# Loads of the gate rows' weights placed behind the weight loads of queries and keys, and forward transforms of a convolution as three rounded products

## The chip, the cores and the metric

The kernel runs on one core of a Trainium2 chip. Its time is the device time of one execution in microseconds; the time before is the median of three. The core has a matrix engine (TensorE, PE in the profile, with its weight loads as PEld), a vector engine (VectorE, DVE), an activation engine (ScalarE, ACT), a general one (GpSimd, POOL), and a sequencer that mostly issues transfers (SyncE, SP). Each engine runs its own instructions in the order in which the program lists them, and semaphores connect them.

## The reference

Two layers work on 256 latent tokens and 256 context tokens of 1024 channels. In both, a token mixer is followed by a squared-ReLU MLP, and each sub-layer is gated and modulated by columns that an adaLN map computes from a conditioning vector:

```python
def adaln(cvec, w, b):
    return jnp.split(jax.nn.silu(cvec) @ w + b, 6, axis=-1)   # shift, scale, gate, twice

def sq_relu_mlp(u, w1, w2):
    return jnp.square(jax.nn.relu(u @ w1)) @ w2
...
x <- LN(ALPHA*x + gate * F(x*(1+scale)+shift))
```

Layer 0's mixer is a conformer convolution: a product to 2048 channels (pw1), a sigmoid gate, a depthwise convolution over 31 taps, layer norm, silu, and a second product (pw2). Context tokens are convolved as one sequence, latent tokens in rows of 64. Layer 1's mixer is a bidirectional chunkwise mLSTM: it makes up-projections (x and z), a short convolution `xc`, values from the former (wv), queries and keys from `xc` (wq, wk), then scores and outputs. All is in 32-bit floats.

## The kernel before

Channels lie on partitions and tokens on the free axis. The order of the work on PE is: pw1, the depthwise convolution, pw2, the four chunks of layer 0's MLP, the up-projections, values, queries and keys (in two pairs of heads, `pair`), attention, and layer 1's MLP.

**Rounded products.** Most matrix products are done as three products of rounded 32-bit operands: each operand is split into a high part, made by a cast on ACT, and a low part, made by a subtraction on DVE (`split`, lines 155 and 156); then come high by high, high by low and low by high (`mm3`, lines 186 to 190). A weight comes in by a 1 MB load on SP's queue into one of three `raw` tiles (`raw_load`, L149); its split gives two `wh` and two `wl` tiles of 128 by 1024, each of which has four buffers.

**The convolution.** The depthwise convolution is done by a transform along the tokens. `turn` (transposes on PE, line 909, and a copy on ACT, line 910) and `vturn3` (a transpose on DVE, a store to memory and a load back, line 904) put the gated tensor with tokens on partitions into `A`. `fwd` (line 926) multiplies `A` by tables of sines and cosines; for the two context tiles (`tt < 2`) it takes windows of the tokens, for which the table `F0` is masked by rows (`ge32`, `lt32`, `ge96`). These are products of plain 32-bit operands, six per half of the channels. `products` multiplies the spectrum by that of the taps, `back` transforms back. The two halves of the channels follow each other, the first at about 69 us, the second at about 135 us.

**The adaLN columns of layer 1.** The class `AdaV` (`step` and `load`, line 420 on) works them out on DVE: each step takes a block `ar` of 256 KB of the transposed map, loaded on SP's queue (L446) into one of two buffers, multiplies it by the row of conditioning values and sums (L439: one custom instruction and one that reads the accumulator). `ada_n1` has units 0 to 3 (32 blocks), `ada_n2` the units 6 to 9, then 4, 5, 10, 11 (64 blocks). The last four are the gates, which two ACT transfers then put into memory as rows (`gate_rows`, L1257). The program calls the steps of `ada_n2` within the loops of values, queries and keys.

**What sets the order.** A scheduler arranges the instructions of each engine; a block in `tc.issue_after(instruction)` is kept behind the instruction named. As nothing holds the `ar` loads, all 96 were moved ahead, into layer 0's MLP, where four or five stand on SP's queue between one weight load and the next.

In that MLP (`mlp`, line 1184 on), PE does for each chunk first the product with w1, whose result passes ACT (relu, L1207), DVE (square, L1208) and a `split` into `hid` (L155, L156), then that with w2. The last chunk's w2 goes through `gemm2` with some of its weights kept in tiles named `u`.

## Time and profile before

| | |
|---|---|
| time, median of 3 runs | 1650.22 us (1646.95 to 1651.23) |
| profiled execution | 1650.45 us |
| its span, first to last instruction | 1648.7 us |
| PE busy | 1623.7 us (98%) |
| DVE busy | 1077.0 us (65%) |
| ACT busy | 728.1 us (44%) |
| mean granted TensorE clock | 0.992 |
| loads `ar`, issued from and to | 164.8 to 509.9 us, 96 of them |

Times are counted from the span's start. A row of the timeline gives start, duration, engine, line and operation, then in brackets how long the engine had been idle and what released it. A row of the windows gives for a stretch the busy time of each engine and the number of instructions, then the granted clock of TensorE (1 is full speed), the share of the DMA engines that was busy, and the GB/s. A row of the waits gives who waited for whom, the total in us, how often, and the longest.

### The profile page before, as it was taken

How to read it: one execution, taken by the hardware profiler on the slowest of the kernel's cores; microseconds unless marked ns; L12 is line 12 of the kernel's file. 1: busy time of each engine (PE TensorE's matmuls, PEld its weight loads, DVE VectorE, ACT ScalarE, POOL GpSimd, SP SyncE). 2: the span in 40 equal slices, each digit the busy share in tenths (PEclk: the TensorE clock that was granted, in tenths of full speed). 3: DMA queues.
4: the chain of work that ended last, by engine and by line, in shares of the span. 5: the costliest groups of instructions: out<-in, count | busy, mean ns of one | idle time of the engine just before them, and what ended most of it. 6: DMA issues, size and time to landing. Idle time of an engine off the chain costs nothing.

```text
span 1648.7 us, 22836 instructions
## 1 busy us (share of the span) xinstructions
PE 1623.7 (98%) x8754; PEld 1356.6 (82%) x8754; DVE 1077.0 (65%) x2052; ACT 728.1 (44%) x1173; POOL 15.2 (1%) x67
## 2 busy tenths in 40 slices
PE   9999999999996999999999999999999999999998
PEld 6675998888885998887777899898888888888887
DVE  7697886986756676763233643453389876787777
ACT  4214763322314376652222532442378654555453
POOL 0000000000000000000000000000000000000001
PEclk9999999999998999999999999999999999999999
DMA  9766233555655157578654632343375566745552
GB/s 361 250 220 239 103 115 128 197 190 193 201 176 153 52 164 226 188 242 281 220 188 149 238 128 103 107 175 131 136 258 187 209 230 203 255 182 190 191 192 90
DMA packets 91069, 306.88 MB, mean 186 GB/s; under 512 B 15020, under 2 KB 33360, under 8 KB 63312
## 3 DMA queue, kind: packets, MB, share of 16 engines
q1 hardware_dynamic: 66416, 289.12, 50.2%
q10 hardware_dynamic: 24544, 16.30, 3.2%
q8 instruction: 69, 1.13, 0.3%
q14 instruction: 40, 0.33, 0.1%
HBM read 287.52 MB, written 17.87 MB: 185 GB/s over the span
## 4 chain that ended last, share of the span: by engine, by line
PE 90%; DMA 6%; DVE 3%; issue 1%; ACT 0%; DVEq 0%; SPq 0%; ACTq 0%
PE mm L186 15%; PE mm L189 15%; PE mm L190 15%; PE mm L202 10%; DMA ar<-adaT_w 4%; PE mm L228 4%; PE mm L230 3%; PE mm L229 3%; PE cv L230 2%; PE cv L228 2%; PE cv L229 2%; PE fl L360 1%; DMA raw<-w 1%; DVE ar L439 1%; PE ln L228 1%; PE ln L229 1%
## 5 line engine op out<-in xcount | busy, mean ns | idle before, releaser
L156 DVE TENSOR_TENSOR wl<-raw,wh 128x1024 fp32r<-128x1024 f32 (+1 forms) x344 | 416.5, 1215 | 255.4 <-ACT wh L155 250.5
L155 ACT CAST wh<-raw 128x1024 fp32r<-128x1024 f32 (+1 forms) x344 | 357.0, 1045 | 458.8 <-PE mm L189 269.0
L189 PE MATMUL mm<-u,wh 128*128 128x512 f32 (+1 forms) x802 | 288.7, 361 | 0.0
L186 PE MATMUL mm<-u,wh 128*128 128x512 f32 (+1 forms) x674 | 239.3, 356 | 0.0
L190 PE MATMUL mm<-u,wl 128*128 128x512 f32 (+1 forms) x674 | 238.1, 355 | 0.0
L189 PEld LDWEIGHTS mm<-u,wh 128*128 128x128 f32 x802 | 151.2, 189 | 23.0 <-issue 0.8
L186 PEld LDWEIGHTS mm<-u,wh 128*128 128x128 f32 x674 | 127.2, 189 | 20.5 <-issue 2.4
L190 PEld LDWEIGHTS mm<-u,wl 128*128 128x128 f32 x674 | 127.1, 189 | 18.5 <-issue 0.8
L186 PE MATMUL mm<-hid,wh 128*128 128x512 f32 (+1 forms) x256 | 95.1, 372 | 13.4 <-ACT hid L155 13.3
L186 PE MATMUL mm<-xm,wh 128*128 128x512 f32 x256 | 100.2, 391 | 0.0
L190 PE MATMUL mm<-xm,wl 128*128 128x512 f32 x256 | 99.6, 389 | 0.0
L189 PE MATMUL mm<-hid,wh 128*128 128x512 f32 (+1 forms) x256 | 94.8, 370 | 0.7 <-DVE hid L156 0.7
L190 PE MATMUL mm<-hid,wl 128*128 128x512 f32 (+1 forms) x256 | 94.5, 369 | 0.0
L228 PE MATMUL mm<-wh,xl 128*128 128x512 f32 x208 | 81.5, 392 | 1.0 <-ACT xl L155 1.0
L229 PE MATMUL mm<-wh,xl 128*128 128x512 f32 x208 | 81.2, 390 | 0.0
L230 PE MATMUL mm<-wl,xl 128*128 128x512 f32 x208 | 80.4, 391 | 0.0
L189 PE MATMUL mm<-qq,wh 128*128 128x272 f32 x256 | 73.9, 289 | 0.0
L186 PE MATMUL mm<-qq,wh 128*128 128x272 f32 x256 | 73.5, 288 | 0.0
L190 PE MATMUL mm<-qq,wl 128*128 128x272 f32 x256 | 73.5, 288 | 0.0
L186 PEld LDWEIGHTS mm<-hid,wh 128*128 128x128 f32 x256 | 50.1, 196 | 21.6 <-ACT hid L155 14.1
L1373 DVE SCALAR_TENSOR_TENSOR E<-pad,vecs,E 128x512 f32<-128x512 f32 x64 | 48.0, 750 | 27.3 <-ACT E L1371 26.0
L155 ACT CAST hid<-E 128x256 fp32r<-128x256 f32 (+1 forms) x70 | 33.9, 485 | 67.9 <-DVE E L1208 64.4
(595 smaller groups left out, 3245.9 us busy)
## 6 DMA issues: line engine op xcount, KB each, us to landing
raw<-w SPq DMA_DIRECT2D x64, 1024.0 KB, 4.9
raw<-wo SPq DMA_DIRECT2D x32, 1024.0 KB, 4.9
ar<-adaT_w SPq DMA_DIRECT2D x96, 256.0 KB, 3.0
raw<-ada_w SPq DMA_DIRECT2D x20, 1024.0 KB, 7.4
raw<-wv SPq DMA_DIRECT2D x16, 1024.0 KB, 6.3
raw<-wq SPq DMA_DIRECT2D x16, 1024.0 KB, 4.8
raw<-wk SPq DMA_DIRECT2D x16, 1024.0 KB, 4.8
u<-wqT SPq DMA_DIRECT2D x56, 256.0 KB, 5.7
```

Of the source, the lines that this page charges most:

```text
L155: c = nc.scalar.copy(hi, src)
L156: lastsub[0] = nc.vector.tensor_tensor(lo, src, hi.bitcast(F32), op=ALU.subtract).ins
L186: a = nc.tensor.matmul(ps, wh, xh, start=start, stop=False)
L189: nc.tensor.matmul(ps, wh, xl, start=False, stop=False)
L190: lastmm[0] = nc.tensor.matmul(ps, wl, xh, start=False, stop=stop).ins
L202: nc.tensor.matmul(o_, w_, x_, start=start and i == 0, stop=stop and i == 15)
L228: nc.tensor.matmul(ps, xh, wh, start=start, stop=False)
L229: nc.tensor.matmul(ps, xl, wh, start=False, stop=False)
L230: return nc.tensor.matmul(ps, xh, wl, start=False, stop=stop).ins
L360: a = mark_unit[0] = nc.tensor.matmul(ps[32 * j:32 * j + 32], cs[:, kt, 14 - 2 * v:46 - 2 * v], blocks[kt], start=first and kt < 4, stop=l ...
L439: nc.vector.tensor_tensor_reduce(tmp("S") if s == 0 else w, w, crow[s][half], 1.0, o if half else V(f"ada_b{self.l}", col), op0=ALU.mult, ...
L1373: nc.vector.scalar_tensor_tensor(s2_(acc), pad[:, :, k:k + C], V("w_conv", m * QTAP + k), s2_(acc), op0=ALU.mult, op1=ALU.add)
```

## The change

It has two parts and some smaller moves.

First, the loads of `AdaV` whose unit stands behind the first four in its list, that is the 32 blocks for the gates, are kept behind the last weight load that the program has issued at that point. Their place is thereby in the stage of queries and keys, and their two instructions each on DVE, and the two transfers `g_dr` on ACT, follow them there.

Second, the context's forward transforms become three rounded products. The tables are split into `FH` and `FL`, masked on DVE instead of POOL; `A`'s two context tiles are split into high and low parts (`a_parts`, held in `U` tiles), from the transposes' result in `turn` and from `A` in `a_split`. `fwd` then issues 18 rounded matmuls per half where it issued six plain ones, in a fixed order.

Beside these, the first half of the block `second` is loaded into `F` tiles, since the `U` tiles are taken, two groups of loads are kept behind it, and two orders near the transposes of silu are fixed.

```diff
--- before.py
+++ after.py
@@ -381,7 +381,7 @@
             else:
                 for i in range(4):
                     t = make()
-                    nc.sync.dma_start(t, ada_w[l, u, half, :, i * 512:(i + 1) * 512])
+                    mark["load"] = nc.sync.dma_start(t, ada_w[l, u, half, :, i * 512:(i + 1) * 512]).ins
                     ts.append(t)
         return ts
 
@@ -443,7 +443,8 @@
         def load(self):
             n, kt = divmod(self.i, DT)
             w = adp.tile([P, 512], F32, tag="ar", name=nm("ar"), bufs=2)
-            nc.sync.dma_start(w, adaT_w[self.units[n], kt // 2, kt % 2])
+            with tc.issue_after(loaded[0]) if n > 3 else nullcontext():
+                nc.sync.dma_start(w, adaT_w[self.units[n], kt // 2, kt % 2])
             self.i += 1
             return w
 
@@ -796,18 +797,22 @@
     (nc.vector.tensor_scalar(cf, cf, -1.0 / L, 2.0 / L, op0=ALU.mult, op1=ALU.add))
     nc.vector.tensor_scalar(tab[:, L:3 * L], tab[:, L:3 * L], cf, None, op0=ALU.mult)
 
-    def masked(name, zero):
-        t = padp.tile([P, L], F32, name=name)
-        nc.gpsimd.tensor_copy(t, F0)
-        for a_, b_ in zero:
-            nc.gpsimd.memset(t[a_:b_, :], 0.0)
-        return t
-
-    ge32 = masked("ge32", [(0, 32)])
-    lt32 = masked("lt32", [(32, 64), (64, 128)])
-    ge96 = masked("ge96", [(0, 64), (64, 96)])
-
-    WIN = [[(F0[0:96, :], 0)], [(ge32, 0), (lt32, 1)], [(ge96, 0), (F0[0:96, :], 1)], [(ge32, 1)]]
+    FH, FL = [padp.tile([P, L], F32R, name=n_) for n_ in ("FH", "FL")]
+    split(FH, FL, F0)
+    mc = padp.tile([P, 3], F32, name="mc")
+    for i_, c_ in enumerate((31.5, 95.5)):
+        nc.vector.tensor_scalar(mc[:, i_:i_ + 1], p_, c_, None, op0=ALU.is_gt)
+    nc.vector.tensor_scalar(mc[:, 2:3], mc[:, 0:1], -1.0, 1.0, op0=ALU.mult, op1=ALU.add)
+
+    def masked(name, i_):
+        ts = [padp.tile([P, L], F32R, name=name + n_) for n_ in "hl"]
+        for t, f_ in zip(ts, (FH, FL)):
+            nc.vector.tensor_scalar(t, f_.bitcast(F32), mc[:, i_:i_ + 1], None, op0=ALU.mult)
+        return ts
+
+    ge32, ge96, lt32 = [masked(n_, i_) for i_, n_ in enumerate(("ge32", "ge96", "lt32"))]
+    F96 = [FH[0:96, :], FL[0:96, :]]
+    WIN = [[(F96, 0)], [(ge32, 0), (lt32, 1)], [(ge96, 0), (F96, 1)], [(ge32, 1)]]
     with tc.issue_after(lastload[0]):
         nc.sync.dma_start(bdw, bdw_d.broadcast_to([P, D]))
     behind.__exit__(None, None, None)
@@ -887,7 +892,16 @@
         else:
             vturn3(f, a)
 
-    turns, three = [], []
+    turns, three, aparts = [], [], {}
+
+    def a_parts(h):
+        if h not in aparts:
+            aparts[h] = [[U(F32R) for _ in range(2)] for _ in range(2)]
+        return aparts[h]
+
+    def a_split(h):
+        for t in range(2):
+            split(*[a_[t][:, 0:2 * P] for a_ in a_parts(h)], A[:, t, h * 512:h * 512 + 2 * P])
 
     def vturn3(f, a):
         h, m = divmod(f, 4)
@@ -902,12 +916,16 @@
             if h == 0:
                 with tc.issue_after(loaded[0]):
                     nc.sync.dma_start(A[:, :, 0:2 * P], a_dr[0])
+                a_split(0)
 
     def turn(f, a):
         tr = psum("ln")
         for b in range(4):
             mark["tr"] = nc.tensor.transpose(tr[:, b * P:(b + 1) * P], a[:, b * P:(b + 1) * P], ident).ins
-        nc.scalar.copy(A[:, :, f * P:(f + 1) * P], tr.rearrange("p (b c) -> p b c", b=4))
+        sl = slice(f % 4 * P, f % 4 * P + P)
+        for t in range(2):
+            split(*[a_[t][:, sl] for a_ in a_parts(f // 4)], tr[:, t * P:(t + 1) * P])
+        nc.scalar.copy(A[:, 2:4, f * P:(f + 1) * P], tr[:, 2 * P:4 * P].rearrange("p (b c) -> p b c", b=2))
         if f == 3:
             with tc.issue_after(mark["tr"]):
                 ada_g1.mm(first, range(4, 8))
@@ -926,18 +944,20 @@
     def fwd(h, tt, xfs):
         sl = slice(h * 512, (h + 1) * 512)
         ps_[tt] = [], list(xfs[::-1])
-        for b in (1, 0) if tt < 2 else (0, 1):
+        a = None
+        for b in (0, 1) if tt > 1 and h == 0 else (1, 0):
             if tt < 2:
-                w_ = WIN[2 * tt + b]
+                w_ = [(fm[k], a_parts(h)[q][t]) for k, q in ((0, 0), (1, 0), (0, 1)) for fm, t in WIN[2 * tt + b]]
                 for i, (fm, t) in enumerate(w_):
-                    a = nc.tensor.matmul(xfs[b], fm, A[0:fm.shape[0], t, sl], start=i == 0, stop=i == len(w_) - 1)
+                    with tc.issue_after(a.ins) if a else nullcontext():
+                        a = nc.tensor.matmul(xfs[b], fm, t[0:fm.shape[0], :], start=i == 0, stop=i == len(w_) - 1)
             else:
 
                 def half_():
                     r = slice(64 * b, 64 * b + 64)
                     return nc.tensor.matmul(xfs[b], F0[r, :], A[r, tt, sl], start=True, stop=True,
                                             tile_position=(64 * b, 0))
-                if b == 0:
+                if b == h:
                     a = lead = half_()
                 else:
                     with tc.issue_after(lead.ins):
@@ -1036,6 +1056,7 @@
         if m == 8:
             with tc.issue_after(mark["gate"]):
                 nc.scalar.dma_start(A[:, :, 512:512 + 2 * P], a_dr[1])
+            a_split(1)
         if m == 4:
             blocks = ada_load(0, 5)
             with tc.issue_after(lastmm[0]):
@@ -1079,8 +1100,9 @@
     gemm(pw1, range(6), u, T, pw1_next, pre=pre1, ahead=True)
     for g in range(2):
         pre_pw2(g)
-    last = ada_load(0, 8)
-    second = ada_load(0, 7, U)
+    second = ada_load(0, 7, F, (0,)) + ada_load(0, 7, U, (1,))
+    with tc.issue_after(mark["load"]):
+        last = ada_load(0, 8)
     with tc.issue_after(mark["tr"]):
         ada_mm(ada_s2.ps, second, 1, False, False, range(4))
     for tt in range(2):
@@ -1102,14 +1124,17 @@
     late4 = []
     for i, tag in enumerate("SLSL"):
         late4.append(tmp(tag))
-        nc.sync.dma_start(late4[i], ada_w[0, 9, 1, :, i * 512:(i + 1) * 512])
+        with tc.issue_after(mark["load"]):
+            nc.sync.dma_start(late4[i], ada_w[0, 9, 1, :, i * 512:(i + 1) * 512])
     more += late4
     with tc.issue_after(mark["fwd", 2]):
         ada_mm(ada_s2.ps, last, 2, False, False)
         ada_mm(ada_s2.ps, more, 3, False, False)
     lead2 = [psum(), psum("cv")]
-    with tc.issue_after(mark_unit[0].ins):
+    filled = {0: mark_unit[0].ins}
+    with tc.issue_after(filled[0]):
         ada_mm(ada_s2.ps, second, 1, False, False, range(4, 8))
+    filled[2] = mark_unit[0].ins
     sact = {0: [], 1: []}
 
     def silu(s):
@@ -1120,9 +1145,10 @@
                 if s == 0 and f == 4:
                     with tc.issue_after(mark["turn", 3]):
                         gate2_sums()
+                    filled[4] = mark_unit[0].ins
                 for i in (1, 3, 0, 2):
                     k = f + i // 2
-                    with tc.issue_after(mark_unit[0].ins) if s == 0 and f == 4 else nullcontext():
+                    with tc.issue_after(filled[f]) if s == 0 and f < 6 else nullcontext():
                         mark["turn", k] = nc.tensor.transpose(tr[:, i * P:(i + 1) * P],
                                                               Y[2 * s + i % 2][k // 4][:, k % 4 * P:k % 4 * P + P], ident).ins
             y = tmp("S")[:, LO]
```

**SP at the end of layer 0's MLP.** `raw` are weight tiles, `w_0` the MLP's weights; the number in a name counts the tiles, which differs by some between the kernels. Before, the last three weight loads and what stands ahead of them:

```order
L446 DMA ar_9807<-adaT_w 128x512
L446 DMA ar_9868<-adaT_w 128x512
L149 DMA raw_4663<-w_0 128x2048
L446 DMA ar_9953<-adaT_w 128x512
L446 DMA ar_10060<-adaT_w 128x512
L446 DMA ar_10169<-adaT_w 128x512
L446 DMA ar_10276<-adaT_w 128x512
L446 DMA ar_10385<-adaT_w 128x512
L149 DMA raw_4727<-w_0 128x2048
L446 DMA ar_10492<-adaT_w 128x512
L446 DMA ar_10601<-adaT_w 128x512
L149 DMA raw_4823<-w_0 128x2048
```

Now, the weight loads of the same place:

```order
L149 DMA raw_4294<-w_0 128x2048
L447 DMA ar_8105<-adaT_w 128x512
L149 DMA raw_4358<-w_0 128x2048
L149 DMA raw_4437<-w_0 128x2048
L149 DMA raw_4513<-w_0 128x2048
L149 DMA raw_4589<-w_0 128x2048
L149 DMA raw_4663<-w_0 128x2048
L149 DMA raw_4728<-w_0 128x2048
L149 DMA raw_4792<-w_0 128x2048
L149 DMA raw_4888<-w_0 128x2048
```

The blocks `ar` between the weight loads are gone from there, but for one.

**SP and DVE at the start of the queries.** `xc_8128` before is `xc_8193` now: the eight subtractions into `xc` make the low parts of the last quarter of the input of the queries and keys; `rk` are rows of gate weights, `res` is the transposed values' tile. DVE before:

```order
L156 TENSOR_TENSOR wl_8233<-raw_8202,wh_8232 128x1024
L1414 STREAM_TRANSPOSE res_8037<-vt_8071 128x16x32
L156 TENSOR_TENSOR xc_8128<-raw_8126,xc_8128 128x256
L156 TENSOR_TENSOR xc_8129<-raw_8126,xc_8129 128x256
L156 TENSOR_TENSOR xc_8134<-raw_8126,xc_8134 128x256
L156 TENSOR_TENSOR xc_8135<-raw_8126,xc_8135 128x256
L156 TENSOR_TENSOR xc_8140<-raw_8126,xc_8140 128x256
L156 TENSOR_TENSOR xc_8141<-raw_8126,xc_8141 128x256
```

DVE now:

```order
L156 TENSOR_TENSOR wl_8298<-raw_8267,wh_8297 128x1024
L1440 STREAM_TRANSPOSE res_8102<-vt_8136 128x16x32
L439 ISA ar_8372,ada_94<-ar_8372,L_2806,ada_94 128x512
L439 ISA ada_94 128x1
L439 ISA ar_8433,ada_94<-ar_8433,L_2805,vecs 128x512
L439 ISA ada_94 128x1
L156 TENSOR_TENSOR xc_8193<-raw_8191,xc_8193 128x256
L156 TENSOR_TENSOR xc_8194<-raw_8191,xc_8194 128x256
L156 TENSOR_TENSOR xc_8199<-raw_8191,xc_8199 128x256
L156 TENSOR_TENSOR xc_8200<-raw_8191,xc_8200 128x256
L156 TENSOR_TENSOR xc_8205<-raw_8191,xc_8205 128x256
L156 TENSOR_TENSOR xc_8206<-raw_8191,xc_8206 128x256
```

SP now, at that place:

```order
L149 DMA raw_8267<-wq 128x2048
L447 DMA ar_8325<-adaT_w 128x512
L149 DMA raw_8330<-wq 128x2048
L1488 DMA rk<-wg_d 128x256
L447 DMA ar_8372<-adaT_w 128x512
L149 DMA raw_8375<-wq 128x2048
L447 DMA ar_8433<-adaT_w 128x512
L149 DMA raw_8438<-wq 128x2048
```

Two blocks now stand on DVE ahead of the first `xc` subtraction; the second of them, `ar_8433`, stands on SP behind two weight loads and `ar_8372`.

## The prediction

> **What bounds the kernel now.** I read the page's first and fourth parts, then PE's waits, then the stretches around the one large wait, then what released it.
>
> ```profile
> PE 1623.7 (98%) x8754; PEld 1356.6 (82%) x8754; DVE 1077.0 (65%) x2052; ACT 728.1 (44%) x1173; POOL 15.2 (1%) x67
> ...
> PE 90%; DMA 6%; DVE 3%; issue 1%; ACT 0%; DVEq 0%; SPq 0%; ACTq 0%
> ```
>
> PE is busy for 98% of the span. So an edit can pay in two ways: by removing PE's own work, or by filling the few places where it stands still. The waits (engine, line waited for, us in total, times, longest) say where these are:
>
> ```profile
> PE mm L186 <- ACT hid L155: 13.3, 2, 12.1
> PE cv L180 <- DVE ones L139: 1.1, 1, 1.1
> ```
>
> One wait of 12.1 us stands out, and the next is 1.1. Its place is the end of layer 0's MLP. In windows (PE's busy us and instructions first, then the other engines; behind them the granted clock, the DMA share and GB/s):
>
> ```profile
> 510.00:520.00 10.00, 9.90 (x51) 8.27 (x49) 8.14 (x14) 5.09 (x9) 0.00 (x0) 1.00 0.37 125
> 520.00:530.00 10.00, 0.60 (x3) 0.30 (x2) 2.22 (x3) 1.10 (x2) 0.00 (x0) 0.67 0.66 89
> 530.00:535.00 5.00, 1.64 (x6) 1.35 (x7) 3.02 (x5) 3.67 (x7) 0.00 (x0) 0.50 0.58 243
> 535.00:540.00 5.00, 3.77 (x18) 3.47 (x18) 2.88 (x7) 1.09 (x2) 0.00 (x0) 0.50 0.76 257
> 540.00:550.00 10.00, 10.00 (x71) 10.00 (x71) 2.99 (x7) 0.00 (x0) 0.00 (x0) 0.81 0.20 83
> 550.00:560.00 10.00, 10.00 (x84) 9.95 (x83) 7.01 (x18) 3.13 (x8) 0.00 (x0) 1.00 0.00 0
> ```
>
> PE's idle time there is 0.10 + 9.40 + 3.36 + 1.23 = 14.1 us. Moreover the clock fell to half, and the work done at half clock lost as much again as full speed would have taken less: 0.2 + 0.82 + 1.89 us up to 540, and then 13 of 84 matmuls in 10 us (1.5 us) to 0.19 of 10 us (1.9 us). The place costs 14.1 + 4.4 to 4.8, about 18.6 us.
>
> Why does PE stand? Timeline rows of SP, DVE and ACT, and the chain of waits:
>
> ```profile
> 495.35 0.33 SPq L149 DMA_DIRECT2D raw<-w  x1
> 496.63 9.85 SPq L446 DMA_DIRECT2D ar<-adaT_w  x5
> 507.28 0.33 SPq L149 DMA_DIRECT2D raw<-w  x1
> 518.43 0.33 SPq L149 DMA_DIRECT2D raw<-w  x1
> ...
> 505.36 0.75 DVE L439 CUSTOM_DVE_ANT_0 ar<-ar,L,ada 128x512 f32<-128x512 f32 x1 [1.57 <-DMA ar<-adaT_w]
> 506.03 1.22 DVE L156 TENSOR_TENSOR wl<-raw,wh 128x1024 fp32r<-128x1024 f32 x1
> ...
> 520.52 0.59 ACT L1207 ACTIVATE E<-mm 128x512 f32<-128x512 f32 x1
> 531.34 1.14 ACT L155 CAST u<-raw 128x512 fp32r<-128x512 f32 x2 [10.23 <-DMA raw<-w]
> 532.38 0.61 ACT L155 CAST hid<-E 128x512 fp32r<-128x512 f32 x1
> ...
> 507.28 5.47 DMA raw<-w
> 518.43 12.82 DMA raw<-w
> ```
>
> SP needs 9.85 us for five `ar` loads, since each waits for a buffer that DVE frees one step later. DVE in turn stands in front of an `ar` (1.57 us idle) while `wl` waits behind it. So the last weight load went out at 518.43 and needed 12.82 us. The cast of `hid`, on which PE waits, stands on ACT behind the casts `u` of that weight, and so it started at 532.38, although the activation ahead of it was over at 521.1.
>
> **The change part by part: the end of the MLP.** Nearly all `ar` loads leave this place. The last weight load then waits only for its `raw` buffer, and that is freed by the subtraction `wl` of the load three places ahead, which needs a `wl` buffer that PE frees. PE takes 24 matmuls for one `wh`, 24 x 0.227 = 5.4 us by the product's pitch (quoted below as 0.23), so a load is needed every 10.9 us. From the order I place the buffer four `wh` ahead at about 509, cast and subtraction behind it (1.05 and 1.22) and the load at about 511.8. With 5.47 us it lands at 517.3, ahead of the activation at 520.52. The `u` casts are then done before `hid` comes up. The chain that is left is the last activation to the last `hid` subtraction. Its steps are activation 0.59, square 0.7, cast 0.62, subtraction 0.69, with some waiting between them: from 520.52 to about 523.5 or 524. PE's last w1 matmul ends at 519.9, and it has about 2 us of matmuls on the other `hid` tiles, as it did in the 3.77 us of the window 535 to 540. I take 2 us left of the hole, with no drop of the clock. **Gain 18.6 − 2 = about 16.5 us**; bounds 12.5 (the hole is left at 6 us, if the load lands like the one that took 12.82) and 18.6 (nothing left).
>
> The 32 × 0.83 us of DVE work moves too, and is free at its old place as PE bounds the stage.
>
> **The context's transforms.** Chain rows (start, us, what), and DVE's row of the turn before the first half:
>
> ```profile
> 61.82 0.23 PE mm L189
> 66.41 1.00 PE fl L360 x8
> 67.40 0.59 PE ln L909 x4
> 68.99 5.35 PE mm L933 x12
> 135.31 4.92 PE mm L933 x11
> ...
> 66.45 0.75 DVE L882 SCALAR_TENSOR_TENSOR E<-mm,vecs,E 128x512 f32<-128x512 f32 x1 [2.99 <-PE mm L190]
> ```
>
> The six plain matmuls of a half stand as twelve records and take 5.35 us, that is 0.89 each; a rounded one takes 0.23 (0.227 as the mean over a longer run of them). Eighteen take 4.1 us, so 1.25 less per half and 2.5 for both. In the new order the third output needs a product bank that `products` frees on DVE; I put 0.3 us per half on this. The new splits on ACT and DVE must be done before the first matmul. In the first half DVE's own row at 66.45 ends at 67.2, just as PE takes up the transposes at 67.40, so four added subtractions there have some tenths to spare; between 62 and 66.4 the engine is idle for 2.99 us. If this cover is gone, PE waits for up to 1 us. **Gain 1.7 us**, between 2.6 (12 × (0.89 − 3 × 0.227)) and 0. The masks, once on POOL, add about ten small DVE instructions in the setup, with no wait of PE behind them that the trace shows; this and the moved loads of `second` I cost at nothing, hidden by the pw1 product.
>
> **The start of the queries.** Here the moved loads cost. Rows of DVE, SP, ACT and PE, two windows, and the landing times of `raw` (KB, median us) and `ar`:
>
> ```profile
> 913.28 1.23 DVE L156 TENSOR_TENSOR wl<-raw,wh 128x1024 fp32r<-128x1024 f32 x1 [0.90 <-ACT wh L155]
> 914.42 0.70 DVE L1414 STREAM_TRANSPOSE res<-vt 128x512 f32<-128x512 f32 x1
> 918.79 2.77 DVE L156 TENSOR_TENSOR xc<-raw,xc 128x256 fp32r<-128x256 f32 x8 [3.66 <-ACT xc L155]
> 912.40 0.33 SPq L149 DMA_DIRECT2D raw<-wq  x1
> 915.69 9.01 SPq L149 DMA_DIRECT2D raw<-wq  x3
> 915.16 3.09 ACTq L1418 DMA_DIRECT2D v_dr<-res  x4
> 922.59 1.09 PE L202 MATMUL mm<-xc,wh 128*128 128x512 f32 x4
> 924.56 1.08 PE L202 MATMUL mm<-u,wh 128*128 128x512 f32 x4
> 916.00:918.00 2.00, 2.00 (x14) 1.80 (x13) 0.00 (x0) 0.00 (x0) 0.00 (x0) 1.00 1.03 326
> 918.00:920.00 2.00, 2.00 (x12) 1.67 (x10) 1.21 (x4) 1.65 (x6) 0.00 (x0) 1.00 1.03 381
> raw<-wq SPq DMA_DIRECT2D x16, 1024.0 KB, 4.8
> DMA to landing us min/median/max: 2.4/3.0/11.0
> ```
>
> In the new order two `ar` blocks stand on DVE behind the transpose of 914.42 and ahead of the eight `xc` subtractions, and the second one's load stands on SP behind `raw`, `rk`, the first `ar` and another `raw`, so it goes out at about 916.4. From 912.4 on the queues then hold 1.05 MB of `raw`, 1.05 MB of values (`v_dr`, four transfers from 915.16), 0.26 of `ar`, 1.05 and 0.26: 3.67 MB. The DMA engines are full there (share 1.03, 326 and 381 GB/s); at some 355 GB/s this is 10.3 us, so with a start at about 913.3 the block lands at about 923.6. The earliest is 921.5 (the `raw` ahead of it issued at 916 and landing after the median 4.8, and 0.7 for the block's own bytes), the latest 925. After 0.83 us for the block the subtractions begin at 924.4 in place of 918.79: 5.6 us late. PE takes up the first subtraction's result at 922.59, 3.4 us after it was done, and the last at about 924.3, 2.7 us after. What is left is a stall of 5.6 − 2.7 = 2.9 us; I take 3, and 1 for the clock, since a wait of this size is a third of the one at 520 that cost 4.4 to 4.8. **Loss 4 us**, between 0.8 (landing at 921.5) and 7 (landing at 925, with the weights' `wl` behind it late too and the clock's loss as at 520 in part).
>
> By the Trainium skill, "TensorE: Matmul & The Clock Gate", section "HAM oscillation — how this bites in real kernels", idle gaps above some 3.4 us throttle the clock to half; the windows at 520 to 540, with 0.50 behind 9.40 us of idling, agree. By that rule a stall of 3 us would pass just free of it, and one of 4 would not.
>
> **The other moved blocks.** The rest, some 29, stand one behind each load of wq and wk.
>
> ```profile
> 930.00:960.00 30.00, 30.00 (x178) 26.61 (x177) 17.91 (x28) 15.60 (x29) 0.00 (x0) 1.00 0.58 209
> DVE ar L439 <- DMA ar<-adaT_w: 41.8, 22, 7.6
> ```
>
> In the queries DVE is busy for 60% of the time and a weight load comes every 5.6 us, so DVE has 2.2 us to spare per load and 1.4 after the block's 0.83. A quarter more bytes (0.26 on 1.05 MB) bring 209 GB/s to about 260, under the 326 seen. With two `ar` buffers a block has a whole load's time, 5.6 us against a median of 3.0 to land. In the keys a load comes every 16 us. I cost them at nothing. Their cover is this slack; without it see the last rival. The two `g_dr` transfers write single elements and stand near `ar` landings of 11.0 us now; in the keys three `raw` tiles are ahead, which covers such a delay.
>
> **Sum.** Against the profiled execution, 1650.45 us (span 1648.7 and 1.75 around it, which stays): 1650.45 − 16.5 − 1.7 + 4 = **1636 us**. That execution lies 0.2 above the median of the runs shown, so nothing is corrected for.
>
> **The rivals.**
>
> No stall at the queries: the block lands by 920 or so, or the hi parts give PE enough to do. For it, the landing median of 3.0; against it, the full DMA share at just that time. 1650.45 − 18.2 = 1632.
>
> The clock falls at the queries. A stall of 4 us or more, with half clock behind it, adds the 4.4 to 4.8 us of the hole at 520 to 3 us of stall: 1650.45 − 18.2 + 7.6 = 1640. For it, the clock of 0.50 that lasted past 540; against it, that idle time was three times as long.
>
> The hole stays. `hid` still stands behind the `u` casts on ACT. If the last load lands again late, since it waits for a `wl` that DVE makes late or for the up-projection's loads, PE waits as before: 1650.45 − 1.7 + 4 with up to 3 saved, 1649 to 1653, no change that can be told. Against it, the DMA share of 0.37 at 510 to 520, and the 9.85 us of SP that no longer stand ahead.
>
> The context's transforms gain nothing, as their new splits hold PE up by what the matmuls save: 1650.45 − 16.5 + 4 = 1638.
>
> Slower: the moved blocks starve PE through DVE's order in the queries. A block there is issued behind a 1 MB load on the same queue. If it lands with or after that load, DVE stands in front of it with the next `wl` behind it, as the 22 waits of 41.8 us (1.9 each, the longest 7.6) show for the MLP. Over the slack of 1.4 us a wait of 3 to 4 us costs some 1.6 to 2.6 at each of 16 loads of wq, 26 to 42 us in all: 1650.45 − 18.2 + 4 + 26 = 1662. It decides from (18.2 − 4) / 16 = 0.9 us per load beyond the slack. Against it, the DMA share of 0.58 there and a whole load's time of lead.
>
> **How the numbers follow.** Forecast 0.55; no stall 0.15; clock 0.10; transforms without gain 0.05; hole stays 0.06; slower 0.09. Below 0.3%, 5 us, a measurement of this kernel can't tell a change from none. Faster by more than that are the first four, 0.85; same 0.06; slower 0.09. The range goes from all bounds at their good end (18.6 and 2.6 gained, 0 lost: 1629) to all at their bad end (12.5 and 0 gained, 7 lost: 1645). It leaves out the slower rival, the hole that stays, and a few hundredths at each end.
>
> **What would show it.** Right for the hole: no wait of PE on `hid` above 3 us, the windows at 510 to 540 full at clock 1.00, the last `raw` load before up_z issued at about 512 in place of 518.43. Right for the transforms: a chain row of 18 matmuls at each of the two places, some 4.4 us long. Right for the queries: a wait of PE on `xc` of about 3 us near 907 (earlier by the gain), and DVE idle ahead of an `ar` there. The prediction is wrong if PE's waits on `wl` in the queries add up to over 5 us, or if a wait above 6 us stays at the MLP's end.

## The result, and the profile after

The changed kernel takes 1639.08 us, the median of 6 runs (1638.39 to 1639.97), where the kernel before takes 1649.62 us on the same chip (1646.95 to 1651.23): a ratio of 0.9937, 95% interval 0.9925 to 0.995. It is faster by about 10.5 us. The profiled execution's span went from 1648.7 to 1637.5 us, 11.2 us less. 1636 was forecast, within 1629 to 1645.

Three intervals between the same instructions say where the difference lies. From the transposes ahead of the first transform (67.40 before, 67.65 after) to the MLP's first activation (219.2 and 219.1) it is 0.35 us less. From there to the MLP's last update of `x` (585.7 and 566.6) it is 19.0 us less. At the last copy of the values (913.1 and 894.0) the lead is 19.1 us; at the first product of layer 1's last stage (1480.4 and 1469.2) it is 11.2 us, and it stays so to the end. So one place gained 19 us and a later one gave back 7.9.

**The end of layer 0's MLP.** PE's waits of the changed kernel:

```profile
PE mm L202 <- DVE xc L156: 3.6, 1, 3.6
PE cv L180 <- DVE ones L139: 1.1, 1, 1.1
```

The 12.1 us on `hid` are gone, and a wait of 3.6 us on `xc` is new. The windows over the old hole, and SP's and ACT's timeline there:

```profile
515.00:520.00 5.00, 5.00 (x33) 4.53 (x32) 4.55 (x10) 3.21 (x5) 0.00 (x0) 1.00 0.15 33
520.00:525.00 5.00, 5.00 (x42) 4.84 (x41) 2.59 (x5) 0.62 (x1) 0.00 (x0) 1.00 0.96 367
...
476.41 31.14 SPq L149 DMA_DIRECT2D raw<-w  x4
...
518.55 0.59 ACT L1233 ACTIVATE E<-mm 128x512 f32<-128x512 f32 x1
520.54 0.62 ACT L155 CAST hid<-E 128x512 fp32r<-128x512 f32 x1 [1.40 <-DVE E L1234]
```

PE is busy throughout at full clock. The last weight load ends its issue at 507.55 (476.41 + 31.14) in place of 518.76. ACT is idle for 1.40 us, until the square is done, before it casts the last `hid`; before, it stood idle for 10.23 us in front of the weight load, with that cast behind it.

**The transforms.** The chain of waits at the two places, then PE's busy time from 160 to 190 us, first of after and then of before:

```profile
69.23 3.01 PE mm L953 x12
72.31 1.65 PE mm L953 x6
...
135.06 3.05 PE mm L953 x12
138.17 1.66 PE mm L953 x6
...
160.00:190.00 30.00, 29.46 (x235) 27.47 (x234) 25.27 (x74) 17.02 (x37) 0.00 (x0) 1.00 0.25 88
```

```profile
160.00:190.00 30.00, 29.99 (x240) 28.02 (x239) 25.85 (x75) 17.85 (x38) 0.00 (x0) 1.00 0.26 88
```

With the gap between the rows a half takes 4.73 and 4.77 us in place of 5.35: 1.2 us saved in both. Behind them PE now idles for 0.54 us between 160 and 190, where it idled for 0.01.

**The start of the queries.** SP, DVE and PE, and four windows:

```profile
896.46 0.43 SPq L447 DMA_DIRECT2D ar<-adaT_w  x1
896.98 0.38 SPq L149 DMA_DIRECT2D raw<-wq  x1
897.41 1.08 SPq L447 DMA_DIRECT2D ar<-adaT_w  x1
...
900.00 0.75 DVE L439 CUSTOM_DVE_ANT_0 ar<-ar,L,ada 128x512 f32<-128x512 f32 x1 [4.00 <-DMA ar<-adaT_w]
905.74 0.75 DVE L439 CUSTOM_DVE_ANT_0 ar<-ar,L,vecs 128x512 f32<-128x512 f32 x1 [4.99 <-DMA ar<-adaT_w]
906.42 2.77 DVE L156 TENSOR_TENSOR xc<-raw,xc 128x256 fp32r<-128x256 f32 x8
...
907.23 2.81 PE L202 MATMUL mm<-xc,wh 128*128 128x512 f32 x4 [3.61 <-DVE xc L156]
...
905.00:907.00 2.00, 0.00 (x0) 0.00 (x0) 1.26 (x4) 0.00 (x0) 0.00 (x0) 1.00 0.56 167
907.00:909.00 2.00, 1.77 (x3) 0.85 (x3) 2.00 (x7) 0.00 (x0) 0.00 (x0) 0.57 0.00 0
909.00:911.00 2.00, 2.00 (x6) 1.47 (x6) 2.00 (x4) 0.93 (x2) 0.00 (x0) 0.50 0.47 70
...
913.00:915.00 2.00, 2.00 (x12) 1.82 (x11) 2.00 (x6) 1.13 (x5) 0.00 (x0) 0.72 1.03 406
```

DVE stands for 4.00 and then 4.99 us in front of the two blocks. The second was issued at about 898 and used at 905.74; only then do the eight subtractions run, PE waits 3.61 us, and the clock falls to half until about 914.

### The profile page after: what moved, and what is told of

It reads as the page before. It is cut to its first block, busy times and chain, and to the rows that moved or that the text cites. A ratio compares the mean times of both kernels' runs of the same rounds, so it can differ in the third digit from the quotient of the medians.

```text
span 1637.5 us, 22842 instructions
## 1 busy us (share of the span) xinstructions
PE 1622.4 (99%) x8766; PEld 1358.2 (83%) x8766; DVE 1082.8 (66%) x2074; ACT 732.0 (45%) x1186; POOL 12.6 (1%) x59
## 4 chain that ended last, share of the span: by engine, by line
PE 95%; DVE 2%; DMA 1%; ACT 1%; issue 0%; ACTq 0%; DVEq 0%
PE mm L186 18%; PE mm L189 18%; PE mm L190 17%; PE mm L202 10%; PE mm L230 3%; PE mm L228 3%; PE mm L229 3%; PE cv L230 1%; PE cv L228 1%; PE cv L229 1%; PE fl L360 1%; PE ln L228 1%; PE ln L230 1%; PE ln L229 1%; PE ln L186 1%; PE cv L983 1%
## 5 line engine op out<-in xcount | busy, mean ns | idle before, releaser
L189 PEld LDWEIGHTS mm<-u,wh 128*128 128x128 f32 x802 | 151.5, 189 | 22.1 <-DVE u L597 0.3
L186 PE MATMUL mm<-hid,wh 128*128 128x512 f32 (+1 forms) x256 | 93.1, 364 | 0.0
L189 PE MATMUL mm<-hid,wh 128*128 128x512 f32 (+1 forms) x256 | 92.8, 363 | 0.0
L439 DVE CUSTOM_DVE_ANT_0 ar<-ar,L,vecs 128x512 f32<-128x512 f32 x48 | 36.0, 750 | 36.9 <-DMA ar<-adaT_w 36.5
L186 PEld LDWEIGHTS mm<-xm,wh 128*128 128x128 f32 x256 | 48.1, 188 | 13.2 <-issue 2.5
```

Of the source, the lines that this page charges most:

```text
L186: a = nc.tensor.matmul(ps, wh, xh, start=start, stop=False)
L189: nc.tensor.matmul(ps, wh, xl, start=False, stop=False)
L439: nc.vector.tensor_tensor_reduce(tmp("S") if s == 0 else w, w, crow[s][half], 1.0, o if half else V(f"ada_b{self.l}", col), op0=ALU.mult, ...
```

## The experiments

The kernel before ran beside each group on the same chip (medians 1650.7 to 1652.4). Ratios are to it, with 95% intervals.

| run | edit | us | ratio |
|---|---|---|---|
| the change | | 1639.08 | 0.9937 (0.9925 to 0.995) |
| e1 | second part alone | 1650.45 | 0.9994 (0.9984 to 1.0003) |
| e2 | first part alone | 1640.08 | 0.9931 (0.9916 to 0.9946) |
| e3 | change, two sums without their wait | 1632.40 | 0.9884 (0.987 to 0.9899) |
| e4 | change, 16 of 32 blocks moved | 1632.93 | 0.9888 (0.9873 to 0.9903) |
| e5 | change, PE kept at work in the wait | 1639.77 | 0.9931 (0.9915 to 0.9948) |
| e6 | before, blocks on POOL's queue | 1664.03 | 1.0076 (1.0061 to 1.0091) |
| e7 | change, 8 of 32 blocks moved | 1632.62 | 0.9889 (0.9874 to 0.9904) |
| e8 | before, 16 blocks moved | 1633.52 | 0.9894 (0.9879 to 0.9909) |
| e9 | before, both row transfers late | 1637.93 | 0.9921 (0.9902 to 0.994) |
| e10 | change, row transfers early | 1645.87 | 0.9969 (0.9957 to 0.998) |
| e11 | before, second row transfer late | 1643.65 | 0.9954 (0.9943 to 0.9966) |

### The two parts apart: e1 and e2

```diff
-            with tc.issue_after(loaded[0]) if n > 3 else nullcontext():
-                nc.sync.dma_start(w, adaT_w[self.units[n], kt // 2, kt % 2])
+            nc.sync.dma_start(w, adaT_w[self.units[n], kt // 2, kt % 2])
```

This is e1, on the changed kernel; e2 has the opposite edit on the kernel before.

> The changed kernel without the first part: all 96 loads stand in layer 0's MLP again, the context's transforms are the rounded products. Theory: the whole gain comes from the loads, and the transforms' part gives under 1 us, because the two traces agree in time again at the first activation of the MLP (219.2 before, 219.1 after). Expected 1648 to 1651 us, PE's wait on hid at the MLP's end of 11 to 13 us as before. Rival: the new transforms are worth the 1.7 us that were predicted, or the hole closes for another reason: 1648 or less, or the wait gone.

> The kernel before with the first part alone: the 32 gate blocks kept behind the weight loads, the context's transforms in plain products. Theory: as the changed kernel within a us, 1638 to 1641 us, no wait of PE on hid above 1 us, a wait of 3 to 4 us on xc at the queries. Rival: part of the closed hole comes from the other moves: over 1643 us.

e1 took 1650.45 us, not to be told from before, with the wait on `hid` back:

```profile
PE mm L186 <- ACT hid L155: 13.9, 2, 12.7
```

e2 took 1640.08 us, as the change. So the gain and the loss both belong to the first part. The second part's own worth is less than the runs can tell: e1's interval allows a gain of up to 2.6 us. The traces are finer. From the transposes ahead of the first transform to the MLP's first activation it takes 151.8 us in all six kernels with plain transforms, and 151.5 to 151.9 us in the seven with rounded ones, 0.1 less on average. The 0.35 us of the change is the largest of these differences.

### What the queries lose: e3, e4 and e5

e3 leaves both loads at their places and takes away what DVE waits for. Two gate columns are then worked out from another row:

```diff
-                nc.vector.tensor_tensor_reduce(tmp("S") if s == 0 else w, w, crow[s][half], 1.0,
+                nc.vector.tensor_tensor_reduce(*((tmp("S"), crow[s][1 - half]) if len(self.units) == 8 and n == 4 and kt in (3, 4) else (tmp("S") if s == 0 else w, w)), crow[s][half], 1.0,
```

> The changed kernel, where the two sums that stand on DVE ahead of the xc subtractions read a row that is already there in place of their blocks. Both loads still go out at the same places of SP's queue, nothing reads them, and two gate columns are not the right ones. Theory: the loss at the queries is DVE standing in front of a block that lands late, so PE's wait on xc of 3.6 us is gone (under 1 us), the clock stays at 1.00 there, and the time falls by 7 to 8 us to 1631 to 1632 us. Rival: the loss is the transfers themselves, which delay the weights and xc; then the wait stays and the time is 1638 to 1640 us.

It took 1632.40 us, and DVE begins the subtractions as soon as ACT has cast:

```profile
901.16 2.77 DVE L156 TENSOR_TENSOR xc<-raw,xc 128x256 fp32r<-128x256 f32 x8 [4.68 <-ACT xc L155]
```

Both loads still go out, and 6.7 of the 7.9 us are gone. What cost these is DVE's place in line, not the bytes. The two sums stand a few us earlier in DVE's order here, as nothing holds them; they fill time in which DVE was idle.

e4 changes a 3 to a 5, so that only the last 16 blocks are kept back and none stands at the start of the queries:

```diff
-            with tc.issue_after(loaded[0]) if n > 3 else nullcontext():
+            with tc.issue_after(loaded[0]) if n > 5 else nullcontext():
```

> The changed kernel with only the last 16 of the 64 blocks kept behind the weight loads (units behind the sixth in the list), so the MLP's last four weight loads have none between them and none stands at the start of the queries. Theory: the hole comes from the blocks between the last weight loads alone, so it stays closed (PE's waits on hid under 1 us), and the queries start without a wait: 1630 to 1633 us, faster than both kernels. Rival: 16 blocks more in the MLP make its weight loads late again, the wait on hid comes back at 4 us or more: 1636 us or more.

1632.93 us: as e3, and here every sum reads its own block. It is faster than both kernels. PE's longest wait is the 1.1 us at the program's start.

How much of the loss is clock? e5 puts matmuls that nobody reads into the wait:

```diff
+            if heat[0] and not start and i == 12:
+                bank = psum("fl")
+                for _ in range(heat[0]):
+                    with tc.issue_after(prev):
+                        prev = nc.tensor.matmul(bank[:, 0:P], ones, ones, start=True, stop=True).ins
...
+        if h == 0:
+            heat[0] = 14
```

> The changed kernel with 14 plain 128x128 matmuls of a tile of ones, into a bank nobody reads, placed on PE where it waits for xc at the start of the queries. Theory: of the 7.9 us lost there 3.6 are PE idle, about 2 are half clock afterwards and the rest is PE paced by DVE's subtractions. With PE kept at work through most of the wait the clock stays at 1.00, and the time falls by 1.5 to 2.5 us, to about 1637, though the wait is no shorter. Rival: the clock has no part in it; the time stays within 0.5 us of the changed kernel's 1639, with the same 4 us between the wait's end and the next group of products.

The clock stayed up:

```profile
905.00:907.00 2.00, 2.00 (x20) 2.00 (x19) 0.57 (x1) 0.35 (x1) 0.00 (x0) 1.00 0.86 262
907.00:909.00 2.00, 1.33 (x6) 0.60 (x4) 2.00 (x8) 0.00 (x0) 0.00 (x0) 1.00 0.02 5
909.00:911.00 2.00, 1.65 (x7) 1.13 (x7) 2.00 (x5) 0.54 (x2) 0.00 (x0) 1.00 0.27 37
...
PE mm L186 <- DVE wgq L1556: 1.0, 1, 1.0
```

From the first query product to the first key product it took 51.6 us (893.8 to 945.4), the changed kernel 53.2 (893.1 to 946.3) and the kernel before 45.9 (912.2 to 958.1). So the queries lose 7.3 us, 1.6 of it by the clock. The time of the whole did not fall: this kernel's order has a new wait of 1.0 us on `wgq` and started 0.7 us later. The expected 1637 us was missed, and only the trace shows the clock's share.

### What made the hole: e6, e7 and e8

The prediction gave two reasons for the late last load, SP's line and DVE's line. e6 takes the blocks off SP's queue:

```diff
-            nc.sync.dma_start(w, adaT_w[self.units[n], kt // 2, kt % 2])
+            nc.gpsimd.dma_start(w, adaT_w[self.units[n], kt // 2, kt % 2])
```

> The kernel before, with the 96 block loads issued by POOL on its own queue in place of SP's; nothing is moved out of the MLP. Theory A: the weight loads were late because they stood on SP behind block loads that wait for a free buffer; then the hole closes, PE's waits on hid are under 2 us and the time is 1632 to 1636 us. Theory B: what made them late is DVE, which stands in front of a block with the subtraction behind it that frees the next raw tile; then the wait on hid stays at 5 us or more and the time is over 1640 us.

It became slower, 1664.03 us, so SP's line alone was not it. PE's waits on `hid` came to 6.0 us, and its longest is now one of 9.7 us on the activation ahead (L1207). The chain of waits at the end of the MLP:

```profile
519.06 2.94 DMA ar<-adaT_w
522.24 0.57 issue
522.89 1.15 DVE wl L156
524.06 13.92 DMA raw<-w
```

DVE's subtraction `wl` stands behind a block, as theory B has it. But the load issued 1.2 us later takes 13.92 us, with no block load left to compete. That was not explained by either theory, and it is the row that led on.

e7 is e4 with a 6 in place of the 5: only the last 8 blocks are moved, and only the MLP's last two loads are free of blocks.

> The changed kernel with only the last 8 blocks kept behind the weight loads (the last unit in the list): four blocks stand ahead of each MLP load but the last two. Theory: the lateness of the last load is the sum over the loads ahead of it, so with two free loads part of the hole comes back: a wait on hid of 1 to 6 us, 1633 to 1640 us. Rival: only the blocks right ahead of the last load count, and the hole stays closed: 1630 to 1633 us.

1632.62 us, with no wait on `hid`. My theory, a lateness summed over many loads, fell: what stands at the end is enough. But the edit moves more than blocks. The second row transfer `g_dr` needs the sums of the last blocks, so in e4, e7 and e8 it leaves the MLP too (it goes out at 1127 us), and these runs alone don't tell the last blocks from that transfer. e8 is e4's edit on the kernel before:

> The kernel before with the last 16 blocks alone kept behind the weight loads: no rounded products in the context's transforms. Theory: the transforms' part is worth less than 1 us, so this is as quick as the half-moved changed kernel (0.9888 of before): ratio 0.988 to 0.990, 1632 to 1634 us where before is 1651. Rival: it is worth the 1.7 us that were predicted: ratio 0.990 or more.

0.9894 against e4's 0.9888: the same within the intervals, and so the second part adds nothing that these runs can tell.

### The row transfers: e9, e10 and e11

What e6's slow load and that of before have in common is a `g_dr` transfer just ahead, on ACT's queue: at 522.9 in e6, at 516.70 in before. An earlier one of before goes out at 468.74, and a block issued behind it is late:

```profile
468.74 0.43 ACTq L1257 DMA_DIRECT2D g_dr<-ada  x1
473.35 11.03 DMA ar<-adaT_w
484.40 0.75 DVE L439 CUSTOM_DVE_ANT_0 ar<-ar,L,vecs 128x512 f32<-128x512 f32 x1 [7.57 <-DMA ar<-adaT_w]
...
516.70 0.37 ACTq L1257 DMA_DIRECT2D g_dr<-ada  x1
```

The DMA view of the kernel before, 516 to 531 us (packets, queues, and issues with KB and us to landing):

```profile
DMA packets 1216, 1.31 MB, mean 88 GB/s; under 512 B 1056, under 2 KB 1056, under 8 KB 1056
...
q1 hardware_dynamic: 176, 1.31, 50.9%
q10 hardware_dynamic: 1040, 0.00, 3.2%
...
raw<-w SPq DMA_DIRECT2D x1, 1024.0 KB, 12.8
raw<-up_z SPq DMA_DIRECT2D x1, 1024.0 KB, 14.1
g_dr<-ada ACTq DMA_DIRECT2D x1, 4.0 KB, 11.1
```

By the code a row is 1024 elements of 4 bytes, each written by itself; they are nearly all of the 1040 packets of q10. The row takes 11.1 us, and the weight load issued beside it 12.8. The row's own packets took 3.2% of the DMA engines' time in this window and the loads' 50.9%: it is the loads that go slowly while a row is under way. By what means the row slows them these runs don't show. e9 moves nothing but the two row transfers:

```diff
-            nc.scalar.dma_start(g_dr[i].rearrange("(k p) -> p k", p=P), ada[1][:, u:u + 8, 1])
+            with tc.issue_after(anchors[-1]):
+                nc.scalar.dma_start(g_dr[i].rearrange("(k p) -> p k", p=P), ada[1][:, u:u + 8, 1])
```

> The kernel before, with only its two gate-row transfers (g_dr on ACT, each 1024 single elements) held back to the end of the keys; all 96 blocks stay in the MLP. In the trace of before the second one goes out at 516.70, and the weight load behind it takes 12.82 us against a median of 4.9. Theory C: over half of the hole comes from this transfer; the last weight load still goes out at 518 but lands after 5 to 6 us, PE's wait on hid falls from 12 to about 5 us with less time at half clock, and the time is 1640 to 1644 us where before is 1651. Rival: the load is slow because of the blocks around it; the wait stays at 11 us or more and the time at 1649 us or more.

1637.93 us, better than the 1640 to 1644 that were expected and, within the intervals, as fast as the change, with all 96 blocks still in the MLP. Its waits and the last weight load in the chain:

```profile
PE mm L186 <- DVE wgq L1518: 2.0, 1, 2.0
PE mm L186 <- ACT hid L155: 1.9, 1, 1.9
...
512.27 5.10 DMA raw<-w
```

The load went out 6 us earlier as well, at 512.27 in place of 518.43. The MLP's stretch, from its first activation to its last update of `x`, takes 349.4 us (219.8 to 569.2), where it took 366.5 before and takes 347.5 in the change: without the rows 17.1 of the 19.0 us are gone. The run gains less, 13 us, since the rows do harm at their new place too. Both go out at 1145 us, and a load of `wo` behind them is slow (chain of waits, PE's wait, windows):

```profile
1147.23 13.74 DMA raw<-wo
...
1163.94 0.36 PE L186 MATMUL mm<-qq,wh 128*128 128x272 f32 x1 [2.03 <-DVE wgq L1518]
...
1164.00:1165.00 1.00, 1.00 (x6) 1.00 (x7) 1.00 (x2) 0.00 (x0) 0.00 (x0) 0.60 0.00 0
1165.00:1166.00 1.00, 1.00 (x6) 1.00 (x6) 0.76 (x4) 0.00 (x0) 0.00 (x0) 0.50 0.57 66
```

From the last copy of the values to layer 1's last stage e9 takes 571.2 us, 3.9 more than before. e11 holds back the second transfer alone:

```diff
+            with tc.issue_after(anchors[-1]) if i else nullcontext():
```

> The kernel before with only the second gate-row transfer held back to the end of the keys; the first goes out at about 469 us as before. Theory C in parts: the first transfer makes a block land after 11 us and so the last weight load go out 6 us late (518.4 against 512.3 with both held back); the second makes that load take 12.8 in place of 5.1 us. With the second alone held back the load goes out at 518 and lands at about 523.5: PE's wait on hid is 4 to 7 us, the time 1642 to 1645. Rival: the second is all of it; the wait is 2 us as with both held back, the time 1638.

```profile
PE mm L186 <- ACT hid L155: 5.7, 3, 4.0
...
519.25 4.70 DMA raw<-w
```

1643.65 us, as expected. Each transfer has its part. The one at 468.7 makes a block land after 11.03 us, DVE stands in front of it for 7.57, and from there the loads go out 6 us late. The one at 516.7 stretches the last load from 5 to 12.8 us. The MLP's stretch takes 357.5 us here (219.6 to 577.1): in these single traces the second transfer costs 9.0 us and the first another 8.1.

In e4, e7 and e8 the first transfer still goes out at about 468 us and the hole is closed. In e11 the second transfer is away too, and e8 differs from it only in its 16 moved blocks: with no block ahead of the last loads, these make up what the first transfer delays.

Does the transfer make a hole by itself? e10 moves the blocks as the change does, and puts both transfers back to the MLP's end. So that they can go out there they copy columns of layer 0:

```diff
-        for i, u in enumerate((16, 40)):
-            nc.scalar.dma_start(g_dr[i].rearrange("(k p) -> p k", p=P), ada[1][:, u:u + 8, 1])
+            nc.scalar.dma_start(g_dr[i].rearrange("(k p) -> p k", p=P), ada[0][:, u:u + 8, 1])
...
+                if keep and c == 3 and m == 5 and s is None:
+                    with tc.issue_after(mark["relu"]):
+                        gate_rows()
```

> The changed kernel, whose blocks stand in queries and keys, with two gate-row transfers put back into the MLP's end, right behind the activation at about 507.7 us; so that they can go out there they copy gate columns of layer 0, and the rows used later are not the right ones. Theory: late blocks and the transfer make the hole together. Here the last weight load goes out in time at 507.5 and is only slowed to about 13 us, so it lands at about 520.5, where PE needs it within 1 to 4 us: a wait on hid of 0 to 4 us, 1639 to 1643 us. Rival: the transfer alone makes the hole: a wait of 8 us or more, 1648 us or more.

```profile
PE mm L186 <- ACT hid L155: 4.1, 2, 2.2
...
508.20 12.83 DMA raw<-w
...
g_dr<-ada ACTq DMA_DIRECT2D x2, 4.0 KB, 17.8
```

1645.87 us, 6.8 over the change and above the 1643 that were expected. The load went out in time, at 508.20, took 12.83 us again, and PE waited 4.1 us on `hid`; in the window 520 to 530 PE was busy for 5.35 us at a clock of 0.75. The MLP's stretch takes 354.6 us (220.1 to 574.7), 7.1 more than in the change: two rows at once, without the blocks, make over a third of the hole's 19.0 us. The blocks without the rows left 1.9 (e9). So neither makes the whole of it alone; each made the other's delay count.

## Why the prediction was right, and where it was wrong

**What bounds the kernel** was read rightly: PE, with one large wait, whose removal is nearly all of the gain.

**The hole's size was right, its cause was half wrong.** 16.5 us were forecast, up to 18.6; 19.0 were measured for the MLP as a whole (`mlp` starts at line 1200 of the kernel before). The small waits on `hid`, 1.9 us in all, are inside the 14.1 us that the prediction counted, so its size of the hole, 18.6, was right to 0.4, and nothing of it was left. The step that failed is "So the last weight load went out at 518.43 and needed 12.82 us": the sentence charges both numbers to the blocks. The rows shown had a load that takes 4.9 us as the median taking 12.82, in a window with a DMA share of 0.66 at 89 GB/s, and the argument did not ask what moved so little with so much share. It was the row transfer, which the change moves along with the blocks' sums because it needs them. The prediction even named the two transfers, their single elements and the block landing of 11.0 us near them. It costed them at their new place, rightly at nothing, and gave them no price at the old one. With them out of the way (e9) 17.1 of the 19.0 us are gone, and the blocks leave a wait of 1.9 us on `hid`; the load then goes out at 512.27, still 5 us later than the 507.22 of the change, and that part is the blocks'. The forecast of the gain held because the same edit removes both causes, and that is luck.

**The 2 us that should be left of the hole** were zero. PE had enough to do on the other `hid` tiles: these products begin at 517.62, and the last `hid` subtraction ends at 521.9, 4.3 us later, with no wait over 0.2. I had allowed for 2 us of such work. The last load also went out earlier than forecast, at 507.22 and not at 511.8 (the terms given for it, 509 and 1.05 and 1.22, make 511.3).

**The transforms**: 1.7 us forecast, 0.35 measured in the change's trace and 0.1 on average over all. (The terms, 2.5 less 0.3 for each half, make 1.9; the 0.2 between is not accounted for.) Two terms were too good. Eighteen rounded matmuls take 4.7 us a half, not 4.4, since they run at 0.25 and 0.275 us each (3.01 over 12, 1.65 over 6) and not at 0.227. And 0.54 us come back as waits behind them, which I had costed at nothing; one is the 0.3 us that PE waits for `products` at the last transform back.

**The queries**: the mechanism was right, place and cause, and e3 shows it. What happened at the clock is the rival that was given 0.10: the clock did fall to half. Its 1640 us came nearer than the forecast, but not by its terms: the clock cost 1.6 us and not 4.4 to 4.8, and neither had DVE's pace, below. The size was 4 us with a bound of 7, and 7.3 to 7.9 were measured, so the bound was a little too low. The terms: the subtractions were to be 5.6 us late and were 6.7 (906.42 against 918.79 less the lead of 19.1). The slack of 2.7 us was read at the second group of products; the first group needs every second of the eight subtractions, and its four matmuls ran at DVE's pace of 0.7 us, which costs 1.7 us on top of the idle 3.6. The clock was put at 1 us and cost 1.6.

The clock-gate rule of the Trainium skill that the prediction cited ("TensorE: Matmul & The Clock Gate", section "HAM oscillation — how this bites in real kernels") would have let a stall of 3 us pass. The change's stall of 3.61 us agrees with it. e2's does not: there the idle time was 3.22 us, and the clock went to half all the same. Windows of e2, and one of e10:

```profile
904.00:908.00 4.00, 0.78 (x6) 0.58 (x4) 1.72 (x6) 1.52 (x2) 0.00 (x0) 0.88 0.73 236
908.00:912.00 4.00, 4.00 (x9) 2.46 (x10) 4.00 (x10) 1.32 (x2) 0.00 (x0) 0.50 0.32 78
912.00:916.00 4.00, 4.00 (x19) 3.40 (x18) 3.48 (x9) 2.14 (x6) 0.00 (x0) 0.77 1.01 414
...
525.00:526.00 1.00, 0.21 (x2) 0.00 (x0) 1.00 (x2) 0.25 (x1) 0.00 (x0) 0.50 1.44 90
```

e9's wait of 1.9 us at the MLP's end left it at 1.00, but behind e9's wait of 2.03 us it fell to 0.50 (the windows from 1164 us above), and in e10 it stood at 0.50 from 525 us, behind waits of 1.90 and 0.51 us close together. So here the clock fell behind idle times well under 3 us, the measurement decides against the rule, and no single length of a wait parts the two cases by these runs.

**The other moved blocks**, costed at nothing, cost at most 1.3 us: in e3, without the stall, the stretch from the last copy of the values to layer 1's last stage takes 568.6 us against 567.3 before. The rival that they starve PE was rightly held for unlikely.

**The sum**: −19.0 and −0.35 and +7.9, with jitter of some tenths at the start, against −16.5 and −1.7 and +4. An error of 2.5 us on the hole went against errors of 1.4 us on the transforms and 3.9 us on the queries. The forecast of 1636 was 3 us too low, chiefly by the queries.

## What to carry to other kernels

When a transfer takes well over twice its median, look at what else is on the queues before charging the instruction ahead of it: here a window with a high DMA share and few GB/s (0.66 at 89) pointed at small packets. The 4 KB row stored as single elements took 11.1 us to land, more than twice a 1 MB load's 4.9, and its place decides what it costs (e9 gains as much as the change, and pays 3.9 us at the rows' new place). And an instruction that waits for a transfer on an in-order engine should stand behind whatever PE needs next; of the 32 blocks it was enough to move 8, with the row transfer that follows them, and best to keep them away from the start of a stage (e4 and e7, 1632.6 to 1632.9 us).

## What the runs showed that was not expected

One transfer of 1024 elements of 4 bytes took 11.1 us, and a 1 MB load beside it 12.8 in place of 4.7 to 5.1 (13.9 in e6, 13.74 in e9). Two together took 17.8 us at the median in e10 and 11.2 in e9. A queue change that keeps everything else can lose: with the block loads on POOL, where each took 0.54 us to issue, the kernel took 1664 us. What part of that is POOL's issue and what part the late blocks was not taken apart. e5 shows that a stall's half-clock tail is real, 1.6 us, and that keeping PE at work through a wait does not help if the kernel's order then waits elsewhere.
